# Where the moving operands of three matmul groups start in SBUF, and the place of two ScalarE copies in the down units

## The chip, the cores and the metric

The program runs on one core of a Trainium2 chip. The metric is the device time of one execution in microseconds (us). A core has a matmul engine (PE, with its weight loads listed as PEld), VectorE (DVE), ScalarE (ACT), GpSimd (POOL) and a queue for transfers (SP). They run side by side and wait for one another through semaphores; each works through its own instructions in order.

## The reference, cut to what matters

A decoder trunk of two layers over 512 tokens of width 1024. Each layer is a half-weighted feed-forward, a mixer, and a second half-weighted feed-forward:

```python
def swiglu(h, w_gate, w_up, w_down):
    return (jax.nn.silu(h @ w_gate) * (h @ w_up)) @ w_down
...
for l in range(DEPTH):
    x = x + 0.5 * swiglu(rms_norm(x, ffn1_norm[l]), ffn1_w_gate[l], ffn1_w_up[l], ffn1_w_down[l])
    h = rms_norm(x, mix_norm[l])
    a, g, q, k, v = jnp.split(h @ w_in[l], splits, axis=-1)
    conv_out = conv_module(a, g, conv_w[l], conv_b[l], conv_norm[l])
    ...
    diff_out = diff_attention(q, k, v, rel_bias, lam, lam_init, subln_g)
    x = x + jnp.concatenate([conv_out, diff_out], axis=-1) @ w_out[l]
    x = x + 0.5 * swiglu(rms_norm(x, ffn2_norm[l]), ffn2_w_gate[l], ffn2_w_up[l], ffn2_w_down[l])
```

The inner width of a feed-forward is 2816, which is 22 tiles of 128.

## The kernel before, in words

Activations are held transposed: 128 features on the partitions, tokens along the free axis. `x` is eight such tiles of 128x512. Every float32 operand of a large product is split into a high and a low part, hi and lo, and a product is three matmuls: weights hi times features hi, weights hi times features lo, weights lo times features hi (`mm3`, L146, L149, L150; in the units the loop of L394). ScalarE makes the hi parts by copies, VectorE the lo parts by subtracting.

**Feed-forward (`ffn`).** The first 5 of the 22 inner tiles (`PLAIN`) go through plain products: gate and up at 128x512 into `ps_pair`, then the plain stage's down product at 128x512 into `ps_d` (L839). Its features are `hh0` to `hh4` and `hl0` to `hl4`, ten tiles of the pool `fp`. The other 17 tiles are done in two groups (8 and 9 tiles) by a fast scheme of seven half-size products instead of eight: `GateUp` units compute the inner tiles, `Down` units (four to a group, `q` = 0 to 3) multiply them by the down weights. All their matmuls are 128x256. The features of the gate and up products are in `acts`; those of the down products are the inner tiles themselves (`hh`, `hl`, again the same tiles of `fp`) and their sums (`hs`), for which `Gated.part` hands out places: the tile `ht`, then spare ones, `rb` and `s0` to `s4`, then `ssum` and `sq` in the first group, and in the second a slice of `acts` and `ones_r`.

**A unit (`Unit.body`).** A unit owns two PSUM banks, in four halves a, b, c and d of 256 columns. Seven products run in this order: c, d, then the last product of the unit before (`prev.rest()`, into *its* half a), a, b, and the tail (c again, then a again). Between them ScalarE copies finished halves to `keep`: c (L412), a and d (L423), and the last quarter, a after the tail (L444). `prev.rest()` of the next unit writes into the same half a, so PE may start it only when the copy of L444 is done. In the gaps the next unit's weights are made ready: GpSimd forms sums of raw weights (L367 to L370), ScalarE makes hi parts of four blocks A, B, C and D (`nxt.hi`, L377), VectorE the lo parts (`nxt.lo`, L381). A is read after GpSimd's L368. The raw weights are in a ring of five buffers (`wraw`) and one for D (`wraw2`): GpSimd's next L367 waits until VectorE has made D's lo part. `Down` with `q` = 0 has a body of its own.

**Mixer.** `conv_in` and `project` use `acts` at 128x512. Attention features are written by `block_out` to the upper half of `acts` (`ch`, `cl`), and the output product (L1223) runs over the convolution half at 128x512 and then over the attention half in two passes of 256 tokens (`ps_out` at 128x256).

**Order and place.** The program is written in one order and a scheduler moves instructions of each engine within what the data allow; `pinned(..., True)` and `keep_in_program_order` hold an instruction at its written place. Tiles are put into SBUF in the order in which the pools ask for them. `acts` is 64 columns wider than needed, and `split(by)` gives a view of it that starts `by` columns (4 bytes each) later: `split(0)` for the plain stages and the mixer, `split(48)`, 192 bytes later, for the units. In this text the *phase* of an operand is the byte of a partition at which it starts, modulo 256. In the built programs the phases of moving operands are these (weights parts start at phase 64 in both):

| moving operand | used at | phase before | phase after |
|---|---|---|---|
| `acts`, plain stages and mixer | 128x512 | 64 | 64 |
| `acts`, units | 128x256 | 0 | 0 |
| inner tiles 0 to 4, plain stage's down | 128x512 | 0 | 64 |
| inner tiles, down units | 128x256 | 0 | 0 |
| attention features, output product | 128x256 | 64 | 0 |
| sums in `rb` and `ssum` | 128x256 | 64 | 0 |
| sums in `ones_r` | 128x256 | 128 | 0 |
| all other sums | 128x256 | 0 or 32 | the same |

Of the kernel before, what the change touches and what calls it, by code (L numbers as in the profile page):

```python
# [18 lines left out]
P = 128  # L19
# [30 lines left out]
GAP = 6  # L50
NEAR, FAR = 48, 0
MOST, SHIFT = 64, (48, 48, 48, 48)
WRAW = 1040
# [19 lines left out]
def trunk(ctx: ExitStack, tc: tile.TileContext, xt, par, lamv, relb, onehot,  # L73
# [24 lines left out]
    def ring(tag, n=1024):  # L98
        if tag == "wraw":
            return rp.tile([P, WRAW], F32, tag=tag, name=tag, bufs=RING[tag])  # L100
        dt = F32 if "raw" in tag else F32R
        more = FAR if "raw" in tag else 0
        return wp.tile([P, n + more], dt, tag=tag, name=tag, bufs=RING[tag])[:, :n]

# [81 lines left out]
    lead = [[tuple(t[1:]) for t in lead[2 * m : 2 * m + 2]] for m in range(2)]  # L186
    ident = const.tile([P, P], F32, tag="ident", name="ident")
    make_identity(nc, ident)
    mhalf = const.tile([P, 16], F32, tag="mhalf", name="mhalf")
    scalars = [const.tile([P, 4 + CT], F32, tag=f"scalars{l}", name=f"scalars{l}") for l in range(DEPTH)]  # L190
    G.memset(mhalf, -0.5)
# [113 lines left out]
    class Halves:  # L305
# [3 lines left out]

        def __init__(self, fp, pr, r, by):  # L310
            self.hi, self.lo = split(by)
            self.th = fp.tile([P, 3, KT // 2, HS], F32R, tag="th", name="th")
# [44 lines left out]
    class Unit:  # L357
# [49 lines left out]
        def body(self, nxt, prev, prev2):  # L407
# [5 lines left out]
            if nxt:  # L413
                nxt.hi("A")
                nxt.lo("A")
# [25 lines left out]
            for ps, *product in self.tail():  # L441
                self.go(ps, *product)
                if ps is self.a:
                    pinned(S.activation(self.keep[:, 2], self.a, AF.Copy))  # L444
            self.close()
# [233 lines left out]
    class Gated:  # L679

        def __init__(self, fp, pairs, many, by, ahead=False):
            self.by = by
            self.fp, self.pairs, self.many, self.ahead = fp, pairs, many, ahead
            self.hh, self.sums, self.held, self.slots, self.open = {}, [], {}, [], None
# [9 lines left out]
        def part(self):  # L694

            if not self.slots:
                ht = self.fp.tile([P, 3, SEQ], F32R, tag="ht", name="hs")
                self.slots = [lambda n=n: ht[:, n] for n in range(3)]
                tags = [(act, "rb", None)] + [(self.fp, f"s{n}", None) for n in range(5)]
                if not self.ahead:  # L700
                    tags += [(tmp, "ssum", 1), (tmp, "sq", None), (tmp, "sq", None)]
                self.slots += [
                    lambda pool=pool, tag=tag, bufs=bufs: one_tile(pool, tag, F32R, "hs", bufs)
                    for pool, tag, bufs in tags
                ]
                if self.ahead:
                    self.slots += [
                        *(lambda t=t: t[:, KT - 1, :] for t in split(self.by)),
                        lambda: const.tile([P, P + SPACE], F32R, tag="ones_r", name="hs")[:, :SEQ],
                    ]  # L710
            return self.slots.pop(0)()

        def part_ninth(self):
# [75 lines left out]

    def ffn(pr, gu, dn, after, turn, by, lead=None, aside=None):  # L790
        with tc.tile_pool(name="ffn", bufs=1) as fp:
            if by:
                fp.tile([P, by], F32, tag="off", name="off")
            r = halves = None
            held, h = [], Gated(fp, 0, PLAIN, by)
            for m in range(PLAIN):
# [29 lines left out]
                if not halves:  # L826
                    halves = Halves(fp, pr, r, by)
            turn += PLAIN
# [15 lines left out]
            for m0, many, pairs in PARTS[1:]:  # L844
                end = m0 + many == FT
                h = Gated(fp, pairs, many, by, end)
                gates = [GateUp(fp, halves, gu[m0 + n, 0], gu[m0 + n, 1], n, h) for n in range(many)]
# [75 lines left out]
    def mixer(l, pr, after, turn):  # L923
        with tc.tile_pool(name="mix", bufs=1) as mp, tc.tile_pool(name="mt", bufs=2) as mt:
# [100 lines left out]

            ch, cl = acth, actl

            ys = [None] * CT
# [185 lines left out]
            for half, t in ((0, slice(0, SEQ)), (1, slice(SEQ // 2, SEQ)), (1, slice(0, SEQ // 2))):  # L1214
                if t.stop == SEQ:
                    w = [None] * 4 if half else wo
                for m in range(KT):
# [22 lines left out]
    for l in range(DEPTH):  # L1240
# [11 lines left out]

        turn = ffn(pr, gu1[l], dn1[l], then(l, "mix_norm"), 2, SHIFT[2 * l], *((lead, aside) if l == 0 else ()))
        mixer(l, nxt["p"], then(l, "ffn2_norm"), turn)
        ffn(nxt["p"], gu2[l], dn2[l], then(l + 1, "ffn1_norm") if l + 1 < DEPTH else last, 0, SHIFT[2 * l + 1])
        pr = nxt["p"]
# [74 lines left out]
```

## Time and profile before

| | |
|---|---|
| median of 3 runs | 1726.87 us (1726.31 to 1734.05) |
| the profiled execution's own time | 1727.72 us |
| its span from the first instruction to the last | 1725.9 us |
| granted TensorE clock | 1.00 |
| busy: PE, DVE, ACT, POOL | 99%, 81%, 58%, 52% of the span |
| plain stage's down, matmuls at 128x512 | 120 in each feed-forward, 480 in all |
| output product over attention features, at 128x256 | 192 in each layer, 384 in all |

In the views, a row of the timeline gives the start and the duration in us, then the engine, the line, the operation, out<-in and the shapes; idle time of the engine and what ended it stand in brackets. A matmul's duration is longer than the distance to the next one's start, since matmuls overlap; the distance of the starts is what it costs.

### The profile page before, as it was taken

How to read it: one execution, taken by the hardware profiler on the slowest of the kernel's cores; microseconds unless marked ns; L12 is line 12 of the kernel's file. 1: busy time of each engine (PE TensorE's matmuls, PEld its weight loads, DVE VectorE, ACT ScalarE, POOL GpSimd, SP SyncE). 2: the span in 40 equal slices, each digit the busy share in tenths (PEclk: the TensorE clock that was granted, in tenths of full speed). 3: DMA queues.
4: the chain of work that ended last, by engine and by line, in shares of the span. 5: the costliest groups of instructions: out<-in, count | busy, mean ns of one | idle time of the engine just before them, and what ended most of it. 6: DMA issues, size and time to landing. Idle time of an engine off the chain costs nothing.

```text
span 1725.9 us, 30801 instructions
## 1 busy us (share of the span) xinstructions
PE 1711.5 (99%) x12013; PEld 1577.4 (91%) x12013; DVE 1401.0 (81%) x2049; ACT 1000.2 (58%) x1607; POOL 899.8 (52%) x664
## 2 busy tenths in 40 slices
PE   9999999999999999999999999999999999999998
PEld 7899999988788899999988999999887888999998
DVE  6988888968867978888968888888788588788886
ACT  6457566655854446566634665665558354575663
POOL 3156565469763155566403565654787432466653
PEclk9999999999999999999999999999999999999999
DMA  6233333523122233333432333334230232333332
GB/s 231 92 111 111 107 115 99 166 80 101 35 86 86 74 107 102 112 109 111 135 98 74 100 109 111 115 107 148 85 110 26 74 107 74 102 110 110 111 98 87
DMA packets 82931, 177.91 MB, mean 103 GB/s; under 512 B 8951, under 2 KB 30726, under 8 KB 82784
## 3 DMA queue, kind: packets, MB, share of 16 engines
q1 hardware_dynamic: 81184, 174.10, 31.8%
q8 instruction: 94, 1.54, 0.4%
q0 software_dynamic: 1312, 1.67, 0.3%
q14 instruction: 53, 0.43, 0.1%
q10 hardware_dynamic: 288, 0.16, 0.0%
HBM read 173.79 MB, written 3.42 MB: 103 GB/s over the span
## 4 chain that ended last, share of the span: by engine, by line
PE 89%; DVE 6%; ACT 2%; issue 2%; POOL 1%; DMA 1%; DVEq 0%; SPq 0%; ACTq 0%; POOLq 0%
PE ps_pair L394 47%; PE ps_pair L146 6%; PE ps_pair L150 6%; PE ps_pair L149 6%; DVE wlo L381 2%; PE ps_d L150 2%; PE ps_d L149 2%; PE ps_d L146 2%; PE ps_sc L1102 2%; PE ps_out L149 2%; PE ps_out L146 2%; PE ps_out L150 2%; PE ps_pair L978 2%; PE ps_pair L979 2%; PE ps_pair L980 2%
## 5 line engine op out<-in xcount | busy, mean ns | idle before, releaser
L381 DVE TENSOR_TENSOR wlo<-wraw,whi 128x1024 fp32r<-128x1024 f32 (+1 forms) x400 | 504.3, 1268 | 123.2 <-ACT whi L377 118.4
L377 ACT ACTIVATE whi<-wraw 128x1024 fp32r<-128x1024 f32 (+1 forms) x400 | 377.0, 953 | 246.0 <-POOL wraw L368 103.0
L367 POOL TENSOR_TENSOR wraw<-wraw 128x512 f32<-128x512 f32 x100 | 115.9, 1159 | 563.9 <-DVE wlo L381 262.7
L394 PE MATMUL ps_pair<-acts,whi 128*128 128x256 f32 x2240 | 390.8, 277 | 0.0
L394 PEld LDWEIGHTS ps_pair<-acts,whi 128*128 128x128 f32 x2240 | 338.1, 188 | 0.4
L394 PE MATMUL ps_pair<-acts,wlo 128*128 128x256 f32 x1120 | 309.8, 277 | 0.0
L394 PE MATMUL ps_pair<-th,whi 128*128 128x256 f32 x816 | 226.6, 278 | 0.5
L394 PE MATMUL ps_pair<-th,wlo 128*128 128x256 f32 x816 | 225.7, 277 | 0.0
L394 PE MATMUL ps_pair<-tl,whi 128*128 128x256 f32 x816 | 225.7, 277 | 0.0
L109 ACT ACTIVATE whi<-wraw 128x1024 fp32r<-128x1024 f32 (+3 forms) x124 | 123.4, 1001 | 151.8 <-PE ps_pair L149 82.2
L394 PEld LDWEIGHTS ps_pair<-acts,wlo 128*128 128x128 f32 x1120 | 210.8, 188 | 0.0
L149 PE MATMUL ps_pair<-acts,whi 128*128 128x512 f32 x448 | 174.5, 390 | 0.0
L146 PE MATMUL ps_pair<-acts,whi 128*128 128x512 f32 x448 | 173.5, 393 | 0.7 <-ACT whi L109 0.7
L150 PE MATMUL ps_pair<-acts,wlo 128*128 128x512 f32 x448 | 174.0, 390 | 0.0
L368 POOL TENSOR_TENSOR wraw<-wraw 128x512 f32<-128x512 f32 x100 | 161.5, 1615 | 7.6
L370 POOL TENSOR_TENSOR wraw<-wraw 128x512 f32<-128x512 f32 x100 | 159.1, 1591 | 7.8
L394 PEld LDWEIGHTS ps_pair<-th,whi 128*128 128x128 f32 x816 | 153.2, 188 | 1.7 <-ACT keep L444 1.3
L394 PEld LDWEIGHTS ps_pair<-th,wlo 128*128 128x128 f32 x816 | 153.6, 188 | 0.0
L394 PEld LDWEIGHTS ps_pair<-tl,whi 128*128 128x128 f32 x816 | 153.2, 188 | 0.0
L369 POOL TENSOR_TENSOR wraw<-wraw 128x512 f32<-128x512 f32 x100 | 143.5, 1435 | 7.8
L394 PE MATMUL ps_pair<-hh,whi 128*128 128x256 f32 x512 | 141.9, 277 | 0.0
L394 PE MATMUL ps_pair<-hl,whi 128*128 128x256 f32 x512 | 141.7, 277 | 0.0
(214 smaller groups left out, 4127.0 us busy)
## 6 DMA issues: line engine op xcount, KB each, us to landing
wraw<-in_gu SPq DMA_DIRECT2D x172, 512.0 KB, 3.9
wraw<-in_wqkv SPq DMA_DIRECT2D x24, 512.0 KB, 4.0
wraw<-in_wag SPq DMA_DIRECT2D x16, 512.0 KB, 3.7
wraw<-in_wout SPq DMA_DIRECT2D x16, 512.0 KB, 3.6
wraw<-in_dn SPq DMA_DIRECT2D x60, 128.0 KB, 3.1
wraw<-in_dn SPq DMA_DIRECT2D x20, 384.0 KB, 3.3
wraw<-in_dn SPq DMA_DIRECT2D x28, 256.0 KB, 3.2
wraw<-in_dn SPq DMA_DIRECT2D x20, 320.0 KB, 3.1
```

What stands on the lines that cost most here:

```text
L109: S.activation(hi, raw, AF.Copy)
L146: first = T.matmul(ps, wh, xh, start=start, stop=False)
L149: T.matmul(ps, wh, xl, start=False, stop=False)
L150: T.matmul(ps, wl, xh, start=False, stop=stop)
L367: G.tensor_tensor(d, g1, u1, op=ALU.add)
L368: G.tensor_tensor(u1, u2, u1, op=ALU.add)
L369: G.tensor_tensor(m0, g1, u1, op=ALU.add)
L370: G.tensor_tensor(m1, g2, m0, op=ALU.add)
L377: pinned(S.activation(hi, raw, AF.Copy), pin)
L381: pinned(V.tensor_tensor(out=lo, in0=raw, in1=f32(hi), op=ALU.subtract), pin)
L394: mm = T.matmul(ps, l, r, start=first and i == n == 0, stop=False, skip_group_check=True)
L978: T.matmul(ps[n], xh[:, t], wh, start=k == 0, stop=False)
```

## The change

It sets the phases of the table above. The ten tiles of the first five inner tiles become slices of one tile `low`: the plain stage writes and reads them at its start, the units 192 bytes later. `block_out` writes attention features to `split(48)` instead of `split(0)`, and the output product reads them there. `rb` is 48 columns longer and the sums that are put there start 48 columns in; `ssum` loses 48 columns that it had behind it, so that the tiles after it stay where they were, and starts 192 bytes later itself. The tile `off`, which moved all the tiles of `fp`, is gone (`low` takes its part), and three small constants are asked for ahead of `ones_r`. Operations, shapes and counts stay the same on every engine.

The other part sets the order on ScalarE: the copy of the last quarter in a down unit (L444) and, in the unit that follows a down unit, the hi part of the next weights' block A (L414) are held at their written places, so that the copy comes ahead of it.

```diff
-NEAR, FAR = 48, 0
-MOST, SHIFT = 64, (48, 48, 48, 48)
+MOST, LATER = 64, 48
...
+    ident = const.tile([P, P], F32, tag="ident", name="ident")
+    mhalf = const.tile([P, 16], F32, tag="mhalf", name="mhalf")
+    scalars = [const.tile([P, 4 + CT], F32, tag=f"scalars{l}", name=f"scalars{l}") for l in range(DEPTH)]
     ones_r = const.tile([P, P + SPACE], F32R, tag="ones_r", name="ones_r")[:, :P]
...
-        r = act.tile([P, SEQ], F32, tag=tag, name=tag)
+        r = act.tile([P, SEQ + LATER], F32, tag=tag, name=tag)[:, :SEQ]
...
-            self.s = tmp.tile([P, SEQ + NEAR], F32, tag="ssum", name="ssum", bufs=1)[:, :SEQ]
+            self.s = tmp.tile([P, SEQ], F32, tag="ssum", name="ssum", bufs=1)
...
             if nxt:
-                nxt.hi("A")
+                nxt.hi("A", isinstance(prev, Down))
...
                 if ps is self.a:
-                    pinned(S.activation(self.keep[:, 2], self.a, AF.Copy))
+                    pinned(S.activation(self.keep[:, 2], self.a, AF.Copy), isinstance(self, Down))
...
-                tags = [(act, "rb", None)] + [(self.fp, f"s{n}", None) for n in range(5)]
+                self.slots.append(lambda: act.tile([P, SEQ + LATER], F32R, tag="rb", name="hs")[:, LATER:])
+                tags = [(self.fp, f"s{n}", None) for n in range(5)]
...
+        def places(self, n, by):
+            if n < PLAIN:
+                return [self.low[:, k * SEQ + by : (k + 1) * SEQ + by] for k in (2 * n, 2 * n + 1)]
+            return one_tile(self.fp, f"hh{n}", F32R, "hh"), one_tile(self.fp, f"hl{n}", F32R, "hl")
+
         def plain(self, n, us):
-            hi = self.fp.tile([P, SEQ], F32R, tag=f"hh{n}", name="hh")
-            lo = self.fp.tile([P, SEQ], F32R, tag=f"hl{n}", name="hl")
+            hi, lo = self.places(n, 0)
...
         def part_hi(self, n, us):
-            hi = one_tile(self.fp, f"hh{self.spot(n)}", F32R, "hh")
-            lo = one_tile(self.fp, f"hl{self.spot(n)}", F32R, "hl")
+            hi, lo = self.places(self.spot(n), LATER)
...
-            if by:
-                fp.tile([P, by], F32, tag="off", name="off")
+            low = fp.tile([P, 2 * PLAIN * SEQ + LATER], F32R, tag="low", name="low")
...
+            heads = split(LATER)
...
-                S.activation(ch[:, CT:, tq], pt, AF.Copy, scale=gsub[l])
-                V.scalar_tensor_tensor(
-                    cl[:, CT:, tq], pt, gsub[l], f32(ch[:, CT:, tq]), op0=ALU.mult, op1=ALU.subtract
-                )
+                hi, lo = (t[:, CT:, tq] for t in heads)
+                S.activation(hi, pt, AF.Copy, scale=gsub[l])
+                V.scalar_tensor_tensor(lo, pt, gsub[l], f32(hi), op0=ALU.mult, op1=ALU.subtract)
...
-                        mm3(ps, wpart(w[m // 2], (m % 2) * 4 + kk), (ch[:, k, t], cl[:, k, t]), kk == 0, kk == 3)
+                        xh, xl = heads if half else (ch, cl)
+                        mm3(ps, wpart(w[m // 2], (m % 2) * 4 + kk), (xh[:, k, t], xl[:, k, t]), kk == 0, kk == 3)
```

Two places show what the second part moves. The first is ScalarE in the first group's down units of the second feed-forward, from the copy of a and d of one unit to that of the next but one; `whi` of 128x1024 are hi parts of A, B and C, that of 128x512 is D. Before:

```order
L423 ACTIVATE keep<-ps_pair 128x512
L377 ACTIVATE whi<-wraw 128x1024 x2
L444 ACTIVATE keep<-ps_pair 128x256
L412 ACTIVATE keep<-ps_pair 128x256
L377 ACTIVATE whi<-wraw 128x1024
L377 ACTIVATE whi_8332<-wraw_8262 128x512
```

and now:

```order
L421 ACTIVATE keep<-ps_pair 128x512
L375 ACTIVATE whi<-wraw 128x1024
L442 ACTIVATE keep<-ps_pair 128x256
L410 ACTIVATE keep<-ps_pair 128x256
L375 ACTIVATE whi<-wraw 128x1024 x2
L375 ACTIVATE whi_8282<-wraw_8212 128x512
```

The pair of `whi` was C and then A of the next weights; A has moved behind the copy of the last quarter (L444, now L442) and that of c (L412, now L410), directly ahead of B. This happens at 17 places: four in the first group of each of the four feed-forwards (in two of them A stood ahead of both copies, in two between them) and one in the second group of the last.

The second is VectorE at the same place; L656 and L646 finish the unit, L671 and L672 the last product of the unit before. Before:

```order
L381 TENSOR_TENSOR wlo<-wraw,whi 128x1024 x2
L656 TENSOR_TENSOR ps_pair<-ps_pair,keep 128x512
L646 SCALAR_TENSOR_TENSOR x<-ps_pair,x 128x512
L381 TENSOR_TENSOR wlo<-wraw,whi 128x1024
L671 TENSOR_TENSOR ps_pair<-ps_pair,keep 128x256
```

and now:

```order
L379 TENSOR_TENSOR wlo<-wraw,whi 128x1024
L654 TENSOR_TENSOR ps_pair<-ps_pair,keep 128x512
L644 SCALAR_TENSOR_TENSOR x<-ps_pair,x 128x512
L379 TENSOR_TENSOR wlo<-wraw,whi 128x1024 x2
L669 TENSOR_TENSOR ps_pair<-ps_pair,keep 128x256
```

A's lo part has moved behind the end of the unit, next to B's. Apart from line numbers and the new name `low`, the orders on PE, GpSimd and the transfer queue are the same.

More of the change, by code (lines that the diff above doesn't have):

```diff
@@ L101, in ring @@
         dt = F32 if "raw" in tag else F32R
-        more = FAR if "raw" in tag else 0
-        return wp.tile([P, n + more], dt, tag=tag, name=tag, bufs=RING[tag])[:, :n]
+        return wp.tile([P, n], dt, tag=tag, name=tag, bufs=RING[tag])
     def parts_of(raw, hi, lo, eng=None, first=False, pin=False):
@@ L186, in trunk @@
     lead = [[tuple(t[1:]) for t in lead[2 * m : 2 * m + 2]] for m in range(2)]
-    ident = const.tile([P, P], F32, tag="ident", name="ident")
     make_identity(nc, ident)
-    mhalf = const.tile([P, 16], F32, tag="mhalf", name="mhalf")
-    scalars = [const.tile([P, 4 + CT], F32, tag=f"scalars{l}", name=f"scalars{l}") for l in range(DEPTH)]
     G.memset(mhalf, -0.5)
@@ L305, in trunk, with __init__ @@
     class Halves:
-        def __init__(self, fp, pr, r, by):
-            self.hi, self.lo = split(by)
+        def __init__(self, fp, pr, r):
+            self.hi, self.lo = split(LATER)
             self.th = fp.tile([P, 3, KT // 2, HS], F32R, tag="th", name="th")
@@ L679, in trunk, with __init__ @@
     class Gated:
-        def __init__(self, fp, pairs, many, by, ahead=False):
-            self.by = by
+        def __init__(self, fp, low, pairs, many, ahead=False):
+            self.low = low
             self.fp, self.pairs, self.many, self.ahead = fp, pairs, many, ahead
@@ L707, in part @@
                     self.slots += [
-                        *(lambda t=t: t[:, KT - 1, :] for t in split(self.by)),
+                        *(lambda t=t: t[:, KT - 1, :] for t in split(LATER)),
                         lambda: const.tile([P, P + SPACE], F32R, tag="ones_r", name="hs")[:, :SEQ],
@@ L788, in get, with ffn @@
             return hi[:, c], lo[:, c]
-    def ffn(pr, gu, dn, after, turn, by, lead=None, aside=None):
+    def ffn(pr, gu, dn, after, turn, lead=None, aside=None):
         with tc.tile_pool(name="ffn", bufs=1) as fp:
-            if by:
-                fp.tile([P, by], F32, tag="off", name="off")
+            low = fp.tile([P, 2 * PLAIN * SEQ + LATER], F32R, tag="low", name="low")
             r = halves = None
-            held, h = [], Gated(fp, 0, PLAIN, by)
+            held, h = [], Gated(fp, low, 0, PLAIN)
             for m in range(PLAIN):
@@ L826, in ffn @@
                 if not halves:
-                    halves = Halves(fp, pr, r, by)
+                    halves = Halves(fp, pr, r)
             turn += PLAIN
@@ L845, in ffn @@
                 end = m0 + many == FT
-                h = Gated(fp, pairs, many, by, end)
+                h = Gated(fp, low, pairs, many, end)
                 gates = [GateUp(fp, halves, gu[m0 + n, 0], gu[m0 + n, 1], n, h) for n in range(many)]
@@ L1251, in last @@
             nc.sync.dma_start(out[m], x[:, m, :])
-        turn = ffn(pr, gu1[l], dn1[l], then(l, "mix_norm"), 2, SHIFT[2 * l], *((lead, aside) if l == 0 else ()))
+        turn = ffn(pr, gu1[l], dn1[l], then(l, "mix_norm"), 2, *((lead, aside) if l == 0 else ()))
         mixer(l, nxt["p"], then(l, "ffn2_norm"), turn)
-        ffn(nxt["p"], gu2[l], dn2[l], then(l + 1, "ffn1_norm") if l + 1 < DEPTH else last, 0, SHIFT[2 * l + 1])
+        ffn(nxt["p"], gu2[l], dn2[l], then(l + 1, "ffn1_norm") if l + 1 < DEPTH else last, 0)
         pr = nxt["p"]
```

## The prediction

> **What bounds the kernel now.** The first view is the page: the span, and how much of it each engine is busy.
>
> ```profile
> span 1725.9 us, 30801 instructions
> PE 1711.5 (99%) x12013; PEld 1577.4 (91%) x12013; DVE 1401.0 (81%) x2049; ACT 1000.2 (58%) x1607; POOL 899.8 (52%) x664
> ```
>
> PE has work for 99% of the span, so there are two ways to a shorter time: matmuls that follow each other at a smaller distance, and the 14 us in which PE stands still. The second view, PE's groups with shapes kept apart, tells where matmuls of one shape are not alike (the last two numbers are busy us and mean ns of one):
>
> ```profile
> L394 PE MATMUL ps_pair<-acts,whi 128*128 128x256 f32 x2240 | 390.8, 277 | 0.0
> L149 PE MATMUL ps_pair<-acts,whi 128*128 128x512 f32 x448 | 174.5, 390 | 0.0
> L394 PE MATMUL ps_pair<-hh,whi 128*128 128x256 f32 x512 | 141.9, 277 | 0.0
> L394 PE MATMUL ps_pair<-hs,whi 128*128 128x256 f32 x704 | 127.0, 279 | 4.0 <-ACT keep L444 4.0
> L394 PE MATMUL ps_pair<-hs,wlo 128*128 128x256 f32 x352 | 97.8, 278 | 0.0
> L149 PE MATMUL ps_d<-hl,whi 128*128 128x512 f32 x160 | 62.9, 394 | 0.0
> L149 PE MATMUL ps_out<-acts,whi 128*128 128x256 f32 x128 | 36.4, 284 | 0.0
> ```
>
> Put beside the phases of the table above, they make a square. At 128x256, `acts` at phase 0 takes 277 ns and at phase 64 (`ps_out`) 284; at 128x512, `acts` at phase 64 takes 390 and the inner tiles at phase 0 394. It isn't the tile: the same `acts` is on both sides of the first pair, and the inner tiles (`hh`) at phase 0 are among the quick ones at 128x256 and among the slow ones at 128x512. Width and phase decide together, and the two widths want different phases.
>
> What a matmul costs is the distance of starts, from PE's timeline: first row and the row after the last one of four stretches (in the first, the last row itself).
>
> ```profile
> 33.63 0.40 PE L146 MATMUL ps_pair<-acts,whi 128*128 128x512 f32 x1
> ...
> 36.13 0.39 PE L150 MATMUL ps_pair<-acts,wlo 128*128 128x512 f32 x1
> ...
> 63.62 0.39 PE L146 MATMUL ps_d<-hh,whi 128*128 128x512 f32 x1
> ...
> 91.62 0.40 PE L394 MATMUL ps_pair<-acts,whi 128*128 128x256 f32 x2
> ...
> 128.35 0.39 PE L394 MATMUL ps_pair<-acts,whi 128*128 128x256 f32 x2
> ...
> 129.71 0.28 PE L394 MATMUL ps_pair<-th,whi 128*128 128x256 f32 x1
> ...
> 513.78 0.28 PE L146 MATMUL ps_out<-acts,whi 128*128 128x256 f32 x1
> ...
> 533.94 0.40 PE L146 MATMUL ps_pair<-acts,whi 128*128 128x512 f32 x1
> ```
>
> At 128x512: `acts`, 11 distances in 2.50 us, 227.3 ns; the plain stage's down, 120 in 28.00 us, 233.3 ns. At 128x256: units, 12 in 1.36 us, 113.3 ns; output product over attention features, 168 in 20.16 us, 120.0 ns.
>
> The third view is PE's waits: the largest is for the very copy that the change moves (us in total, times, longest).
>
> ```profile
> PE ps_pair L394 <- ACT keep L444: 4.0, 4, 1.4
> ```
>
> **The change, part by part.** *Plain stage's down.* 480 matmuls go from phase 0 to phase 64, where 128x512 runs at 227.3: 480 x (233.3 - 227.3) = 2.9 us. From below the bound is 0 (the slow row goes on), from above 3.2 us (the duration rows differ by 4 ns, the distances by 6.0, and 6.6 is the most that any of these pairs shows). I take 2.9, since width, phase and even the phase of the weights are those of the 227.3 row.
>
> *Attention features.* 384 matmuls go from phase 64 to 0: 384 x (120.0 - 113.3) = 2.6 us, bounds 0 and 2.6.
>
> *Spare sums.* 192 matmuls leave phase 64 and 48 leave phase 128. The `hs` rows are 2 ns (704) and 1 ns (352) above 277, 1.8 us in all, over more matmuls than the 240; at 6.7 ns each the 240 would give 1.6. Bounds 0 and 1.6; I take 0.8, the middle, as part of that excess belongs to rows that stay.
>
> The Trainium skill's page "TensorE: Matmul & The Clock Gate", section "Back-to-back issue gap", gives a warm distance by the width alone, about N/2.4 + 2.5 ns. By that estimate 512 columns cost 215.8 ns and 256 cost 109.2 at any address, and these three terms would be nothing; the rows, 227.3 against 233.3 and 113.3 against 120.0, don't agree.
>
> What hides behind PE in these stretches must follow a little faster. In the plain stage's down of the first feed-forward the other engines have this much to do:
>
> ```profile
> 63.00:92.00 29.00, 29.00 (x128) 23.32 (x127) 26.63 (x38) 12.61 (x18) 9.62 (x8) 1.00 0.23 77
> ```
>
> VectorE, third, is busy for 26.63 of 29.00 us, and the stage shrinks by 120 x 6.0 ns = 0.7: 1.6 us are left, so the term stands. Without them, at most that 0.7 us a feed-forward is lost.
>
> *ScalarE's order.* The timeline round one of the four waits, ScalarE first, then PE:
>
> ```profile
> 728.23 1.06 ACT L377 ACTIVATE whi<-wraw 128x1024 fp32r<-128x1024 f32 x1 [0.22 <-PE ps_pair L394]
> 733.25 1.06 ACT L377 ACTIVATE whi<-wraw 128x1024 fp32r<-128x1024 f32 x1 [3.96 <-POOL wraw L368]
> 734.21 0.37 ACT L444 ACTIVATE keep<-ps_pair 128x256 f32<-128x256 f32 x1
> 734.48 0.38 ACT L412 ACTIVATE keep<-ps_pair 128x256 f32<-128x256 f32 x1
> ```
> ```profile
> 733.45 0.28 PE L394 MATMUL ps_pair<-hs,wlo 128*128 128x256 f32 x1
> 734.63 0.39 PE L394 MATMUL ps_pair<-hs,whi 128*128 128x256 f32 x1 [0.91 <-ACT keep L444]
> ...
> 1063.58 0.28 PE L394 MATMUL ps_pair<-hs,wlo 128*128 128x256 f32 x1
> 1064.56 0.39 PE L394 MATMUL ps_pair<-hs,whi 128*128 128x256 f32 x1 [0.70 <-ACT keep L444]
> ...
> 1587.98 0.28 PE L394 MATMUL ps_pair<-hs,wlo 128*128 128x256 f32 x1
> 1589.62 0.38 PE L394 MATMUL ps_pair<-hs,whi 128*128 128x256 f32 x1 [1.37 <-ACT keep L444]
> ...
> 1700.13 0.40 PE L394 MATMUL ps_d<-hh,nine 128*128 128x512 f32 x1
> 1701.54 0.51 PE L394 MATMUL ps_pair<-hs,whi 128*128 128x256 f32 x2 [1.01 <-ACT keep L444]
> ```
>
> ScalarE stood idle for 3.96 us at A's copy, which waited for GpSimd's L368, with the finished quarter behind it. Its copy needs nothing but PE's tail. Between the tail and 734.63's product stand c and d, 12 matmuls each of 113.3 ns, 2.7 us, and they ended at 733.45 + 0.11: the quarter was finished at 730.8, c at 732.2. In the new order both copies run in that idle time and PE goes straight on. The four distances lose 1.18 - 0.11, 0.98 - 0.11, 1.64 - 0.11 and 1.41 - 0.23, together 4.6 us; the matmul after each restart is about 0.1 us late too (restarting rows last 0.39 for one, not 0.28). That is 5.1 us at most. From below it is a loss, the third rival's. I take 5.1, because A's data arrived at 733.2 while both copies could have been over by 732.6 (c's end and 0.38): A isn't delayed at such a place.
>
> *Where A is delayed.* At the other places A was ready earlier, and it now stands behind both copies, with B and D behind it; GpSimd's L367 waits for D's lo part. ScalarE, VectorE and GpSimd at one:
>
> ```profile
> 208.32 1.06 ACT L377 ACTIVATE whi<-wraw 128x1024 fp32r<-128x1024 f32 x1 [2.78 <-POOL wraw L368]
> 209.56 0.37 ACT L412 ACTIVATE keep<-ps_pair 128x256 f32<-128x256 f32 x1
> 209.95 1.07 ACT L377 ACTIVATE whi<-wraw 128x1024 fp32r<-128x1024 f32 x1
> ...
> 218.67 0.38 ACT L412 ACTIVATE keep<-ps_pair 128x256 f32<-128x256 f32 x1
> ```
> ```profile
> 213.36 0.68 DVE L381 TENSOR_TENSOR wlo<-wraw,whi 128x512 fp32r<-128x512 f32 x1
> ```
> ```profile
> 214.12 1.10 POOL L367 TENSOR_TENSOR wraw<-wraw 128x512 f32<-128x512 f32 x1 [2.51 <-DVE wlo L381]
> 215.30 2.11 POOL L368 TENSOR_TENSOR wraw<-wraw 128x512 f32<-128x512 f32 x1
> ```
>
> A moves from 208.32 to at most 209.9, B from 209.95 to at most 210.9 (one copy later), and D's lo part and GpSimd's L367 by at most the same 0.9 us. Then L368 ends at 218.3 in place of 217.4. The next A is due only after the next copy of c, at 218.67: 0.4 us of cover is left, and A's weights themselves are used only a unit later. So I cost the delay at nothing; without that cover each place would pay up to one copy, 1.06 us.
>
> *Sum* against the profiled execution's own time: 1727.7 - (2.9 + 2.6 + 0.8 + 5.1 = 11.4) = 1716.3 us. That execution lies 0.85 above the median of the runs, so the median should come to 1715.5 us; the times below are on this footing.
>
> **The rivals.** *The stalls return elsewhere.* PE arrives earlier at the next copies and the gap reappears. For it: GpSimd's chain, which held A, keeps its pace, and PE still waits for L444 in gate units, whose order isn't changed. Against it: the wait wasn't for data but for a copy that stood in a queue, and between 734.6 and the next restart PE has no other wait of this size. Then only the 6.3 us of the phases are won: 1720.6.
>
> *The address doesn't set the distance.* If width and weights alone set it, and something else in `ps_d` and `ps_out` made them slow, only the stalls go: 1726.9 - 5.1 = 1721.8. Against it stands the square of rows, above all `acts` on both sides. The Trainium skill's page "SBUF — State Buffer", section "Specifications (TRN2)", speaks for it: full bandwidth needs two hits in a 16-byte line, which contiguous 4-byte columns from any of these starts have. The rows, 277 and 284 ns, don't agree.
>
> *A's delay reaches PE (slower).* Place: A's copy, L414, behind c's copy at 17 places. With one copy of 1.06 us paid at each, 18.0 us are lost against 11.4 won: 1733.5. It turns to slower from 11.4 / 17 = 0.67 us a place. Against it: the 0.4 us of cover after a delay that was reckoned at its largest, and that at the four stalls A isn't delayed at all.
>
> **How the numbers follow.** Forecast 0.75, stalls return 0.13, address without effect 0.07, A's delay 0.05. The forecast's own range is 1713.5 (spare sums at their bound, a little more off the gate units' waits) to 1718.5 (sums at nothing, 2 us of stalls back). The range takes in the first rival: 1713.5 to 1721.0, and leaves out most of the last two. Half a per cent is 8.6 us, about what a measurement of this kernel can tell from no change, so faster means under 1718.2: 0.72 of the forecast and nothing else. Within: 0.03 of the forecast, the first two rivals, 0.23 in all. Slower: 0.05.
>
> **What would show it.** In the profile after: `ps_d` rows at 390 ns and 28.00 us shrunk to 27.3; `ps_out` at 128x256 at 277 and 168 distances in 19.0 us; `hs` at 277 to 278; no wait of PE for the last quarter's copy over half a us, with that copy ahead of A in ScalarE's timeline. The forecast is wrong if `ps_d` stays at 394, if PE's waits in down units move to another name, or if GpSimd's L368 ends later than c's copy and A's copy leads to a wait of PE.

## The result and the profile after

The change made the kernel slower: 1741.01 us median of 5 runs (1740.54 to 1742.72) against 1726.87 us (5 runs beside it, 1724.95 to 1734.05), a ratio of 1.0077 [1.0055, 1.0099]. The prediction was 1715.5 us and a gain. The profiled execution after took 1740.85 us, 13.1 us more than the one before (1727.72).

The page after, span and engines:

```profile
span 1739.1 us, 30788 instructions
PE 1729.0 (99%) x12013; PEld 1600.8 (92%) x12013; DVE 1393.4 (80%) x2049; ACT 998.5 (57%) x1607; POOL 887.3 (51%) x664
```

PE stands still for 10.1 us instead of 14.4 (span less busy time), yet the span is 13.2 us longer. So no wait took the time: PE itself got slower. Its groups with shapes kept apart (busy us, mean ns of one, idle before) say where:

```profile
L392 PE MATMUL ps_pair<-acts,whi 128*128 128x256 f32 x2240 | 403.1, 281 | 0.0
L392 PE MATMUL ps_pair<-th,whi 128*128 128x256 f32 x816 | 229.3, 281 | 0.0
L392 PE MATMUL ps_pair<-hs,whi 128*128 128x256 f32 x704 | 126.7, 279 | 0.0
L147 PE MATMUL ps_d<-low,whi 128*128 128x512 f32 x160 | 62.1, 389 | 0.0
```

`ps_d` fell from 394 to 389 ns, as forecast. But the 2240 unit matmuls from `acts`, which the change doesn't touch (same tile, same phase 0, same phase of the weights), rose from 277 to 281.

PE's timeline after, the rows at the ends of its stretches (start us first):

```profile
63.30 0.39 PE L144 MATMUL ps_d<-low,whi 128*128 128x512 f32 x1
...
90.50 0.40 PE L392 MATMUL ps_pair<-acts,whi 128*128 128x256 f32 x2
...
130.08 0.28 PE L392 MATMUL ps_pair<-th,whi 128*128 128x256 f32 x1
...
306.75 0.40 PE L392 MATMUL ps_pair<-hh,nine 128*128 128x512 f32 x1
...
308.88 0.39 PE L392 MATMUL ps_pair<-low,whi 128*128 128x256 f32 x2
...
310.24 0.39 PE L392 MATMUL ps_pair<-hs,whi 128*128 128x256 f32 x2
...
513.98 0.28 PE L144 MATMUL ps_out<-acts,whi 128*128 128x256 f32 x1
...
516.10 0.28 PE L144 MATMUL ps_out<-acts,whi 128*128 128x256 f32 x1
...
517.24 0.28 PE L144 MATMUL ps_out<-acts,whi 128*128 128x256 f32 x1
...
537.03 0.39 PE L144 MATMUL ps_pair<-acts,whi 128*128 128x512 f32 x1
...
1380.97 0.28 PE L144 MATMUL ps_out<-acts,whi 128*128 128x256 f32 x1
...
1400.01 0.39 PE L144 MATMUL ps_pair<-acts,whi 128*128 128x512 f32 x1
```

From the first unit matmul to the same `th` row, 336 distances later, went 38.09 us before (91.62 to 129.71) and go 39.58 us now: 113.4 against 117.8 ns each, and at 117.8 it stays up to the *ninth products* at 306.75 (the plain 128x512 products of the second group's ninth inner tile); behind them, from 308.88 to 310.24, 12 distances take 113.3 each. The output product over attention features runs the same 168 matmuls from the same addresses in both layers: 19.79 us in the first (117.8 ns), 19.04 us in the second (113.3). One address, one width, two paces, in one execution. In both layers the first 19 matmuls of this product, ahead of the 168, stand right behind 128x512 products at phase 64 and take 117.8 ns each (in the first layer 513.98 to 516.10, 18 distances). Then come four 128x128 matmuls, and behind those only the second layer is quick.

The same two paces stood in the trace of before. Its timeline round a short stall of PE in the first feed-forward, and the first ninth product behind it:

```profile
130.73 0.28 PE L394 MATMUL ps_pair<-th,whi 128*128 128x256 f32 x1
130.85 0.28 PE L394 MATMUL ps_pair<-tl,whi 128*128 128x256 f32 x1
130.96 0.28 PE L394 MATMUL ps_pair<-th,wlo 128*128 128x256 f32 x1
131.15 0.39 PE L394 MATMUL ps_pair<-th,whi 128*128 128x256 f32 x1
...
131.61 0.28 PE L394 MATMUL ps_pair<-th,whi 128*128 128x256 f32 x1
...
132.55 0.28 PE L394 MATMUL ps_pair<-th,wlo 128*128 128x256 f32 x1
...
302.92 0.40 PE L394 MATMUL ps_pair<-hh,nine 128*128 128x512 f32 x1
```

From 129.71 (a row of the prediction) to 130.96, eleven distances, 113.6 ns each; from 131.61 to 132.55, eight distances, 117.5. It goes on like this to 187.8 us. Call the paces quick (113.3) and slow (117.8). The granted clock doesn't make them: it was 1.00 in the quick stretch from 92 to 130 us and in the slow one from 132 to 187, as in the changed kernel's slow one from 91 to 300.

Where the 13.1 us come from: units up to the first ninth product take 216.25 us in the first feed-forward now (306.75 - 90.50) against 211.30 (302.92 - 91.62), and over all four 865.0 against 844.2, +20.8 (three of the four waits for L444 lay in those 844.2 and are gone). The plain stage's down gives 4 x (28.00 - 27.20) = 3.2 back, the attention features 2 x 20.16 - 19.79 - 19.04 = 1.5. The remaining -3.0 lies for the most part (-2.7) in the last 36 us of the feed-forwards, behind the first ninth product, where the stall at 1700.13 is gone and the stream is quick for longer.

### The profile page after: what moved, and what is told of

Same layout as the page of the kernel before. It is cut to its first block, busy times and chain, and to the rows that moved or that the text cites. A ratio compares the mean times of both kernels' runs of the same rounds, so it can differ in the third digit from the quotient of the medians.

```text
span 1739.1 us, 30788 instructions
## 1 busy us (share of the span) xinstructions
PE 1729.0 (99%) x12013; PEld 1600.8 (92%) x12013; DVE 1393.4 (80%) x2049; ACT 998.5 (57%) x1607; POOL 887.3 (51%) x664
## 4 chain that ended last, share of the span: by engine, by line
PE 96%; DVE 3%; DMA 1%; ACT 0%; issue 0%; DVEq 0%; SPq 0%; ACTq 0%
PE ps_pair L392 54%; PE ps_pair L144 6%; PE ps_pair L148 6%; PE ps_pair L147 6%; PE ps_d L147 2%; PE ps_d L144 2%; PE ps_d L148 2%; PE ps_sc L1104 2%; PE ps_out L144 2%; PE ps_out L148 2%; PE ps_out L147 2%; PE ps_pair L981 2%; PE ps_pair L979 2%; PE ps_pair L980 2%; PE ps_o L1134 1%; PE ps_v L1009 1%
## 5 line engine op out<-in xcount | busy, mean ns | idle before, releaser
L379 DVE TENSOR_TENSOR wlo<-wraw,whi 128x1024 fp32r<-128x1024 f32 (+1 forms) x400 | 488.6, 1232 | 137.4 <-ACT whi L375 129.4
L365 POOL TENSOR_TENSOR wraw<-wraw 128x512 f32<-128x512 f32 x100 | 120.7, 1206 | 592.9 <-DVE wlo L379 311.7
L392 PE MATMUL ps_pair<-acts,whi 128*128 128x256 f32 x2240 | 403.1, 281 | 0.0
L392 PEld LDWEIGHTS ps_pair<-acts,whi 128*128 128x128 f32 x2240 | 342.9, 188 | 0.3
L392 PE MATMUL ps_pair<-acts,wlo 128*128 128x256 f32 x1120 | 314.6, 281 | 0.0
L392 PE MATMUL ps_pair<-tl,whi 128*128 128x256 f32 x816 | 229.3, 281 | 0.0
L392 PE MATMUL ps_pair<-th,wlo 128*128 128x256 f32 x816 | 229.3, 281 | 0.0
L367 POOL TENSOR_TENSOR wraw<-wraw 128x512 f32<-128x512 f32 x100 | 151.2, 1512 | 7.8
L366 POOL TENSOR_TENSOR wraw<-wraw 128x512 f32<-128x512 f32 x100 | 149.6, 1496 | 7.6
L368 POOL TENSOR_TENSOR wraw<-wraw 128x512 f32<-128x512 f32 x100 | 145.7, 1457 | 7.8
L392 PE MATMUL ps_pair<-hs,whi 128*128 128x256 f32 x704 | 126.7, 279 | 0.0
L1072 DVE SCALAR_TENSOR_TENSOR ps_y<-u,par,ps_y 128x512 f32<-128x512 f32 x156 | 117.6, 754 | 3.8
```

The costliest lines, as they stand in the source:

```text
L365: G.tensor_tensor(d, g1, u1, op=ALU.add)
L366: G.tensor_tensor(u1, u2, u1, op=ALU.add)
L367: G.tensor_tensor(m0, g1, u1, op=ALU.add)
L368: G.tensor_tensor(m1, g2, m0, op=ALU.add)
L379: pinned(V.tensor_tensor(out=lo, in0=raw, in1=f32(hi), op=ALU.subtract), pin)
L392: mm = T.matmul(ps, l, r, start=first and i == n == 0, stop=False, skip_group_check=True)
```

## The experiments

The theories. **M, memory**: the 128x256 stream has two paces and keeps the one it has until something disturbs it. Before, 512-wide products at phase 0 led into the units and left them quick; now products at phase 64 do and leave them slow. **O, order**: the pinned copies, or the stalls that they took away, make it slow. **A, addresses**: the new places of the units' other tiles (`th`, `tl`, `keep`) do.

The last column counts slow unit matmuls in the profiled execution: those whose distance, averaged with the next two in PE's timeline, is over 115.5 ns. Some 8,330 can be classed so in each kernel. Ratios are against the kernel before, run beside each on the same chip.

| kernel | us, median | ratio [95%] | slow |
|---|---|---|---|
| before | 1726.87 | 1 | 1474 |
| the change | 1741.01 | 1.0077 [1.0055, 1.0099] | 7373 |
| e1_plain0 | 1730.76 | 1.0014 [1.0001, 1.0028] | 4081 |
| e2_kick64 | 1733.97 | 1.0040 [1.0025, 1.0054] | 5586 |
| e3_order | 1723.37 | 0.9974 [0.9964, 0.9985] | 1168 |
| e4_last0 | 1724.52 | 0.9983 [0.9971, 0.9994] | 2919 |
| e5_all0 | 1726.33 | 0.9985 [0.9968, 1.0002] | 3018 |
| e6_last64 | 1746.79 | 1.0111 [1.0098, 1.0124] | 7390 |
| e7_phases | 1741.57 | 1.0081 [1.0065, 1.0097] | 7388 |
| e8_allpin | 1719.59 | 0.9955 [0.9943, 0.9968] | 191 |
| e9_copy_first | 1720.65 | 0.9948 [0.9933, 0.9963] | 1073 |
| e10_last64_apart | 1745.76 | 1.0091 [1.0078, 1.0105] | 7368 |

**e1_plain0: the plain stage back at phase 0.**

```diff
-            hi, lo = self.places(n, 0)
+            hi, lo = self.places(n, LATER)
```

> The changed kernel with one edit: the plain stage's inner tiles are back at phase 0 (the 480 ps_d matmuls at 128x512), all else stays. Theory M (memory): the 128x256 stream at phase 0 has two paces, 113.3 and 117.7 ns, and keeps the one it begins with until something disturbs it; a 512-wide product at phase 0 ahead of it starts it at 113.3, one at phase 64 at 117.7, and a 256-wide matmul at phase 32 turns it to 117.7. It expects units to start at 113.3 and stay there till the first sum at phase 32 (about 94 us later, some 770 matmuls in each feed-forward), then 117.7: -13.5 us, +3.2 us for ps_d back at 233 ns, together about 1731 us. Theory O (the two pinned copies, or the stalls that they took away, made the stream slow) and theory A (the new addresses of the units' tiles th, tl, keep and of their weights made it slow): units stay at 117.7 from the first one on, and ps_d costs 3.2 us more: about 1744 us.

1730.76 us, where M said 1731 and the others 1744. Units began quick in all four feed-forwards. They fell to the slow pace at 130.5 us (first) and 1513 us (fourth) behind a short stall, at 710.5 us (second) at the first sum at phase 32, and in the third not at all. M had expected the fall at the first sum at phase 32 in all four, so its pace at the start was right and its total in part luck. O and A fall: with the pins and the new addresses in place the units can be quick.

**e4_last0: one inner tile alone.** Of the five inner tiles only the last, whose three matmuls stand right ahead of the units.

```diff
-            hi, lo = self.places(n, 0)
+            hi, lo = self.places(n, LATER if n == PLAIN - 1 else 0)
```

> The changed kernel with one edit: only the last of the plain stage's five inner tiles is at phase 0 (96 of the 480 ps_d matmuls, among them the three right ahead of the units), all else stays. Theory M (memory): what stands right ahead of the units sets their pace, so units start at 113.3 ns and stay there till the first sum at phase 32, some 770 matmuls in each feed-forward: -13.5 us, and +0.6 us for 96 matmuls at 233 ns: about 1728 us. A variant of it, that the whole stage before sets the pace, expects 117.7 ns. Theory O (pinned copies) and theory A (addresses of the units' other tiles): no change but the 96 matmuls, 1741 to 1742 us.

1724.52 us, 16.5 below the change, 3.5 better than M's sum (the sums at phase 32 turned the stream in the second feed-forward alone; in the two of the second layer they left it quick). Its timeline:

```profile
90.33 0.39 PE L147 MATMUL ps_d<-low,whi 128*128 128x512 f32 x1
90.56 0.39 PE L148 MATMUL ps_d<-low,wlo 128*128 128x512 f32 x1
90.79 0.40 PE L392 MATMUL ps_pair<-acts,whi 128*128 128x256 f32 x2
...
128.89 0.28 PE L392 MATMUL ps_pair<-th,whi 128*128 128x256 f32 x1
```

336 distances in 38.10 us: quick. Three matmuls of 512 columns at phase 0 right ahead of the units are enough, with twelve at phase 64 in front of them.

**e6_last64 and e10_last64_apart: the reverse.** The stage at phase 0 but for its last inner tile. In e6_last64 that tile began on the end of the one before it and overwrote it, so part of the feed-forward is computed from overwritten columns; e10_last64_apart, whose edit follows, lays the tiles apart.

```diff
-            hi, lo = self.places(n, 0)
+            hi, lo = self.places((n + 1) % PLAIN, LATER if n < PLAIN - 1 else 0)
```

> e1_plain0 (plain stage at phase 0, 1730.8 us, units begin at 113.3 ns) with one edit: the last of the five inner tiles is at phase 64, where its 96 matmuls are quicker by 6.6 ns (-0.6 us). Theory M: the product right ahead of the units sets their pace, so they start at 117.7 and stay there to the end of the first group's down units: 1741.0 + 3.2 - 0.6 = 1743.6 us, some 13 us slower than e1_plain0 though the edited matmuls themselves are quicker. If the stage as a whole, or the share of its matmuls at phase 0, sets the pace: 1730 us.

> The same question as e6_last64 with the inner tiles apart from each other (there the last tile began on the end of the one before it, so that part of the feed-forward's product was that of overwritten columns): four inner tiles of the plain stage at phase 0, the last, whose 3 matmuls stand right ahead of the units, at phase 64. Theory M: units start at 117.7 ns in each feed-forward: 1743.6 us by the sum, or 1746.8 as e6_last64 measured. If the stage as a whole sets the pace: 1730 us as e1_plain0.

1746.79 and 1745.76 us. The timeline of e10_last64_apart:

```profile
63.18 0.39 PE L144 MATMUL ps_d<-low,whi 128*128 128x512 f32 x1
...
90.64 0.40 PE L147 MATMUL ps_d<-low,whi 128*128 128x512 f32 x1
90.88 0.39 PE L148 MATMUL ps_d<-low,wlo 128*128 128x512 f32 x1
91.11 0.40 PE L392 MATMUL ps_pair<-acts,whi 128*128 128x256 f32 x2
...
130.68 0.28 PE L392 MATMUL ps_pair<-th,whi 128*128 128x256 f32 x1
```

39.57 us for the same 336: slow, in all four feed-forwards. The stage with the edit is no longer than without (27.93 us, 63.18 to 91.11, against 28.00), yet the kernel is 0.8% slower than e1_plain0 by the ratios (1.0091 and 1.0014). Not the stage, but what stands right ahead of the units, sets their pace. The 96 matmuls won only 0.07 us a feed-forward, 3 ns each in place of 6.6: where phases alternate, a 512-wide product doesn't keep its own price either.

**e2_kick64: one spare sum back at phase 64.**

```diff
-tag="rb", name="hs")[:, LATER:])
+tag="rb", name="hs")[:, :SEQ])
```

> The changed kernel with one edit: the one spare sum in rb is at phase 64 again (128 matmuls), all else stays. Theory M (memory): a phase-64 matmul of 256 columns turns the stream back to 113.3 ns. Units start at 117.7 ns as in the changed kernel; within the down units of the first group the pace alternates (117.7 after each sum at phase 32, 113.3 after each one in rb); after the last of them, about 220 us, it stays at 113.3 for some 740 matmuls in each feed-forward: about -15 us, 1726 us. Theory O (pinned copies) and theory A (addresses of the units' other tiles): units stay at 117.7 throughout and the 128 matmuls cost up to 0.9 us more: 1741 to 1742 us.

1733.97 us: 7 us better than the change, 8 us short of M's number. In the first layer it went as M says. The timeline at the first such sum (the row at 186.59 holds two matmuls, the first at phase 64 and the second at phase 0; the one at 186.83 is at phase 64 again):

```profile
186.00 0.28 PE L392 MATMUL ps_pair<-hl,whi 128*128 128x256 f32 x1
186.12 0.28 PE L392 MATMUL ps_pair<-hh,wlo 128*128 128x256 f32 x1
...
186.59 0.40 PE L392 MATMUL ps_pair<-hs,whi 128*128 128x256 f32 x2
186.83 0.28 PE L392 MATMUL ps_pair<-hs,wlo 128*128 128x256 f32 x1
...
187.64 0.39 PE L392 MATMUL ps_pair<-low,whi 128*128 128x256 f32 x2
187.86 0.28 PE L392 MATMUL ps_pair<-low,wlo 128*128 128x256 f32 x1
187.98 0.28 PE L392 MATMUL ps_pair<-low,whi 128*128 128x256 f32 x1
```

Slow before (0.12 from row to row), quick behind (three distances in 0.34 from 187.64). The pair at 186.59 took 0.24 us, 0.01 more than a quick one, and six matmuls later the stream was quick, which won 4.4 ns for each matmul that followed. In the second layer the same sums took 113 to 115 ns and turned nothing: the units there stayed slow up to the ninth product. So such a matmul can turn the stream, and not always does; what decides it is open.

**e3_order: the kernel before with the order alone.**

```diff
-                nxt.hi("A")
+                nxt.hi("A", isinstance(prev, Down))
...
-                    pinned(S.activation(self.keep[:, 2], self.a, AF.Copy))
+                    pinned(S.activation(self.keep[:, 2], self.a, AF.Copy), isinstance(self, Down))
```

> The kernel before with only ScalarE's order changed (both copies pinned in down units), no phase changed. Theory M (memory): units start at 113.3 ns in each feed-forward as before; the four waits for the last quarter's copy go (-4.6 us): about 1722 us, with up to 2 us either way where a stall that used to turn the pace is gone. Theory O (the pinned copies or the missing stalls make the stream slow): units at 117.7 ns as in the changed kernel, about 1741 us less what the sums at phase 64 turn back: over 1730 us. Theory A (addresses): about 1722 us, the same as theory M.

1723.37 us; against the 1727.47 beside it 4.1 won, and 4.9 between the two profiled executions (1722.80 and 1727.72). Units began quick in all four feed-forwards, so the pins don't make them slow. So this half of the change wins by itself, but less by its waits than was forecast: of the 4.9, PE's idle time gives 2.7 (14.4 to 11.7 us; the waits for L444 fell from 4.0 to 0.3, and other short waits grew), and 306 fewer slow matmuls at 4.4 ns give about 1.3, by estimate.

**e7_phases: the change without the order.** The two edits of e3_order undone in the changed kernel.

> The changed kernel without ScalarE's order: phases alone. Theory M: units start at 117.7 ns as in the changed kernel; the order's waits may come back, but at the slower pace PE leaves ScalarE more time, so they are smaller than the 4.6 us before, and a wait may turn the pace back to 113.3: 1736 to 1745 us. Theory O (the pinned copies or the missing stalls made the stream slow): units at 113.3, the prediction's sum without the order's term, 1720.6 us.

1741.57 us, ratio 1.0081, the same as the change's 1.0077 within their intervals. So all of the loss is that of the phases, and in their presence the order wins nothing that can be measured. PE's waits there:

```profile
PE ps_pair L392 <- ACT keep L442: 0.6, 1, 0.6
```

One wait of 0.6 us, where there were four, 4.0 us in all, at the quicker pace of before: with the phases changed and the old order, most of the stalls are gone. That the slower PE leaves ScalarE the time fits this and was expected, but no run shows it apart.

**e5_all0: no address in the units but phase 0.** e4_last0, and the spare buffer of the squares at phase 0 instead of 32.

```diff
+    wp.tile([P, 16], F32, tag="pad", name="pad", bufs=1)
...
-            sq = self.s if k == 0 else tmp.tile([P, SEQ + 8], F32, tag="sq", name="sq")[:, GAP : GAP + SEQ]
+            sq = self.s if k == 0 else tmp.tile([P, SEQ], F32, tag="sq", name="sq")
```

> The changed kernel with its last inner tile of the plain stage at phase 0 (as in e4_last0) and with the second spare buffer moved from phase 32 to phase 0 (no gap ahead of the squares, 64 bytes of filling behind them), so that every 256-wide matmul of the units starts at phase 0 and a 512-wide product at phase 0 leads them in. Theory M: units start at 113.3 ns and no address turns them any more; e4_last0 ran 2919 matmuls of units at 117.7, of them 1034 behind the second feed-forward's sum at phase 32 (-4.5 us: 1720 us), and 1485 behind a stall of 0.07 us at 130.3 us (another -6.5 us if the stall doesn't come back: 1713.5). Between 1713 and 1720 us. If sums at phase 32 turn nothing: 1724.5 us as e4_last0.

1726.33 us, worse than expected, and 12 runs from 1716.04 to 1733.75, the widest spread here. In the profiled execution the first two feed-forwards were quick throughout, and the last two slow for 1485 matmuls each, behind a stall at 980.7 and 1508.8 us. It is the stall at 130.3 us of e4_last0 at its place in each feed-forward; in the first feed-forward it left the stream quick here and slow there:

```profile
129.80 0.28 PE L393 MATMUL ps_pair<-th,whi 128*128 128x256 f32 x1
129.91 0.28 PE L393 MATMUL ps_pair<-tl,whi 128*128 128x256 f32 x1
130.03 0.28 PE L393 MATMUL ps_pair<-th,wlo 128*128 128x256 f32 x1
130.21 0.39 PE L393 MATMUL ps_pair<-th,whi 128*128 128x256 f32 x1
130.44 0.28 PE L393 MATMUL ps_pair<-tl,whi 128*128 128x256 f32 x1
130.56 0.28 PE L393 MATMUL ps_pair<-th,wlo 128*128 128x256 f32 x1
130.67 0.28 PE L393 MATMUL ps_pair<-th,whi 128*128 128x256 f32 x1
130.79 0.28 PE L393 MATMUL ps_pair<-tl,whi 128*128 128x256 f32 x1
130.90 0.28 PE L393 MATMUL ps_pair<-th,wlo 128*128 128x256 f32 x1
```

A stall of 0.07 us, less than a matmul, and then either pace for 1485 matmuls, up to 6.5 us. That this is what spreads the runs fits their range (four feed-forwards, each one way or the other), but only one of them was profiled.

**e8_allpin: that stall taken away.** e5_all0 with the copy pinned ahead of A's weights in gate units too.

```diff
-                nxt.hi("A", isinstance(prev, Down))
+                nxt.hi("A", prev is not None)
...
-                    pinned(S.activation(self.keep[:, 2], self.a, AF.Copy), isinstance(self, Down))
+                    pinned(S.activation(self.keep[:, 2], self.a, AF.Copy), True)
```

> e5_all0 with ScalarE's order pinned in gate units too (last quarter's copy ahead of A's weights everywhere), to take away the short stall at 130.3 us, which in e1_plain0 and e4_last0 turned the first feed-forward's units from 113.3 to 117.7 ns for 1485 matmuls. Theory M: without the stall the pace stays at 113.3, -6.5 us against e5_all0 if that one still has the stall, about 1713 us; if the delay of A's weights reaches PE, up to one copy of 1.06 us a gate unit is lost. If the stall isn't what turns the pace: as e5_all0.

1719.59 us (1718.34 to 1722.60), 0.9955 of before: clearly faster than both kernels. Its groups and PE's largest wait:

```profile
L393 PE MATMUL ps_pair<-acts,whi 128*128 128x256 f32 x2240 | 389.2, 276 | 0.0
L393 PE MATMUL ps_pair<-th,whi 128*128 128x256 f32 x816 | 226.3, 277 | 3.1 <-ACT keep L534 3.1
```
```profile
PE ps_pair L393 <- ACT keep L534: 3.1, 8, 0.5
```

Only 191 slow matmuls are left, and 276 ns where the change has 281. Against e5_all0's profiled execution (1726.36 us, 3018 slow) the pace should have won 2,827 x 4.4 ns = 12.4 us; 8.0 were won (1718.34), as eight new stalls (L534, 3.1 us) came and the waits for `nine` (L718) grew from 0.4 to 1.6 us: PE, quicker now, waits at the hand-over between the groups and at the ninth products. The 1713 us that M gave left these out.

**e9_copy_first: those eight stalls taken away.** e8_allpin with `nxt.hi("C")` behind the copy of the last quarter in those two units.

> e8_allpin with one more piece of order: in the two gate units of a feed-forward that stand next to the hand-over between groups, ScalarE copies the last quarter ahead of the next unit's C weights too (there PE waited 0.5 to 0.7 us for that copy, eight times in e8_allpin). Theory M: the pace stays near 113.3 ns as in e8_allpin and the eight stalls of 3.1 us in all, with up to 0.1 us of restart each, go: about 1716 us. If C's weights, made one copy later, are then waited for, nothing is won: 1719 to 1722 us.

1720.65 us, 0.9948 [0.9933, 0.9963] (the kernel before took 1730.49 beside it), not told apart from e8_allpin. The waits for L534 are gone. In their place PE stopped once in each feed-forward among the spare sums of the first down unit (one distance of 0.28 to 0.34 us); the stop at 1039.05 us left 981 matmuls slow.

## Why the prediction was wrong

**The step that failed** is the square of rows: "Width and phase decide together". In the long stretches of 128x512 products they did (227.3 and 233.3 ns before, 226.7 after). At 128x256 and phase 0 there are two paces, and the sum rested on the units keeping the quick one, which it took from 12 distances behind 128.35 us and never named as a condition: it has no term for the matmuls that the change leaves alone. What had kept them quick were two of the things that the change removed. The plain stage's down at phase 0, worth 2.9 us in the sum as a fault, led the units into the quick pace in four feed-forwards of four; at phase 64 it led them into the slow one in four of four. And the spare sums at phase 64, worth 0.8 as a fault, brought the stream back in the first layer when it had fallen (e2_kick64, where 128 of them at phase 64 again won 7.0 us). Slow unit matmuls went from 1474 to 7373. At 4.4 ns each, the difference of the paces, that is 26 us by estimate, against 11.4 hoped for.

The trace of before had the sign of it. The `hs` rows' excess over 277 was laid to the 240 matmuls off phase 0. With these moved the mean is still 279 in the changed kernel, now from the slow pace, and it falls to 277 in e8_allpin, which is quick and has no sum off phase 0: a mean of 279 doesn't tell an address from a pace. Sums stood in the slow stretch up to 187.8 us of before too, so a part of the excess was the pace. And one view more, the timeline behind the stall at 130.96 us, showed phase 0 at 117.5.

Point by point:

- *Plain stage's down*, 2.9 us: right; 27.20 us instead of 28.00 in the first feed-forward, 226.7 ns each, 3.2 in all.
- *Attention features*, 2.6 us: mis-sized. Over the 168 of each layer 0.37 us in the first and 1.12 in the second, as the first ran slow.
- *Spare sums*, 0.8 us: wrong in sign, above.
- *ScalarE's order*, 5.1 us: near it alone (4.1 to 4.9 in e3_order), but in part by luck, as some 1.3 of that was the pace; nothing that can be measured at the slow pace (e7_phases). The terms weren't independent.
- *A's delay*, nothing: right. No wait of PE in the changed kernel's units names A's weights or the last quarter's copy, and none names A's weights in e3_order, at the quick pace.
- *VectorE's cover*: it held, the stage shrank by 0.8 us.

The rivals: *the stalls return* didn't happen in the change (no wait for `keep` is left). *The address doesn't set the distance* is nearer than it looked, as the same addresses gave 113.3 and 117.8, but its number was that of a gain, and `ps_d` did follow its address. *A's delay* was the only rival on the other side and has no part in it. None had the mechanism; the sign that was left with 0.05 came about.

The Trainium skill's page "TensorE: Matmul & The Clock Gate", section "Back-to-back issue gap", says that in a stream of weight loads and matmuls the spacing is set by both, and gives its figures by the width alone; the formula in the prediction is its figure for an isolated matmul. The weight loads do differ between the paces (below), which fits the first part without showing it; 113.3 and 117.8 ns at one width, in one execution, don't agree with figures by the width alone.

## What to carry to other kernels

Before a price is put on moving an operand, check that the rows beside it, which the change doesn't touch, have one pace: a mean of 277 or 279 ns may be a mixture of two, and then what stands ahead of a long stream can be worth more than the operands moved. Where the stream keeps a pace, choose the product right ahead of it and remove the short stalls within it (e8_allpin), and price terms together, since a stall that is taken away at one pace may not exist at the other.

## What the hardware showed

- Two self-keeping paces of 128x256 matmuls at phase 0, each with its own weights: 113.3 and 117.8 ns. The slow one ran unbroken over some 1,830 distances in each of the four feed-forwards of the changed kernel. The weight loads tell them apart as well; first the changed kernel from 100 to 180 us, then e8_allpin from 100 to 170:

```profile
L392 PEld LDWEIGHTS ps_pair<-acts,whi 128*128 128x128 f32 x250 | 38.2, 188 | 0.0
L392 PEld LDWEIGHTS ps_pair<-acts,wlo 128*128 128x128 f32 x126 | 24.2, 192 | 0.0
```
```profile
L393 PEld LDWEIGHTS ps_pair<-acts,whi 128*128 128x128 f32 x230 | 34.7, 188 | 0.0
L393 PEld LDWEIGHTS ps_pair<-acts,wlo 128*128 128x128 f32 x115 | 21.6, 188 | 0.0
```

- In the slow pace the load of `wlo` lasts 192 ns, in the quick one 188; that of `whi` 188 in both. Whether that is the cause or a trace of it no run here tells.
- What turned the pace: the product ahead (with 512 columns at phase 0 all 28 entries into units of the seven kernels that have it were quick, at phase 64 all 20 of the other five slow), some 256-wide matmuls at phase 64 (to quick) and phase 32 (to slow), and stalls as short as 0.07 us, which left it either way. All these products stood ahead of units at phase 0, so no run tells whether phase 64 itself or the difference from the units' phase makes them slow. Why a stall falls one way or the other, and why the sums of the second layer turn nothing, stays open.
- Behind a stall, phase 0 ahead isn't enough. A feed-forward's first ninth products are six 128x512 matmuls from an inner tile at phase 0, with PE stopping among them for 0.2 us or more. In the twelve kernels 42 of the 48 left the stream quick, all four of the changed kernel among them, and six left it slow; in five of these six the last of the six matmuls took 226 ns itself, in e7_phases for example at 1172.5 us, where long stretches at phase 0 take 233. So a 512-wide product doesn't keep one price at one phase either.
